# A planned kernel gets 192-column index projections, a plan in which VectorE and GpSimd exclude each other, and 64x64 products held together

## The chip, the cores and the metric

The kernel runs on one core of a Trainium2 chip. The metric is the time of one execution on the device in microseconds; the time of a kernel is the median of its runs. Besides, one execution was recorded by the profiler; spans, durations and waits below are of that one.

## The reference

Two layers work on 256 tokens of 2048 channels. Each normalises x, projects it by one wide matrix, and gives the columns to three branches: A (a Mamba-2 scan), B (RWKV-7 time mixing, a delta rule with a 64x64 state per head, 16 heads) and C (sparse attention). Gated sums of the three are projected once more and added to x. What the change touches is branch C's indexer: 16 small heads score each key for each query, and only the best top_k = 64 keys are attended to:

```python
top_k = min(TOPK_MAX, S // 4)            # 64 for S = 256
logits_idx = jnp.einsum('bqhd,bsd->bqhs', iqb, ik)
score = jnp.einsum('bqh,bqhs->bqs', iwb, jax.nn.relu(logits_idx))
score = jnp.where(causal[None], score, -jnp.inf)
_, sel = lax.top_k(score, top_k)
```

The mask is causal, so query t has t + 1 keys. Queries 0 to 63 have at most 64 and get all of them, whatever the scores.

## The kernel before

Activations lie transposed, channels on partitions and the 256 tokens along the columns. Every float32 weight and activation is split into a high and a low part (type fp32r), and a product is three: high x high, high x low, low x high (`acc`). Weights stream from memory into `wraw`, 128 x 1024 at a time; `prepare` makes halves of 512 columns from it, on ScalarE (ACT) the high part `whi` and on VectorE (DVE) `wlo = wraw - whi`. `block` runs the products of one block of 128 output channels: 16 chunks of 128 input channels, three products each, the weights stationary and `hh` or `hl`, the activations, moving. `unit` does two blocks into one PSUM tile `psg`, of which there are 3. One half of weights serves 12 products. These long products are most of TensorE's (PE's) work.

The small products of the branches go to PSUM tiles `psa` (5 of them). After each half, `pump` advances the chains ("lanes") of the branches by a step in the program's order. Branch B has for each pair of head pairs a serial part, `rwkv_chunk`: for two halves of a chunk, four 64x64 float32 products, one for each head, with the inverse (`ut`) as stationary operand; a copy of all four by ScalarE; then four with `b_nm` (the correction), which VectorE adds to X, two heads at a time. Branch C's index part: four units of index queries (`proj_c`), each rotated by `rope` on VectorE and GpSimd (POOL), then for each of the 16 heads `index_scores` on the rotated tile, and `select`, which finds the 64 best by eight rounds of max and replace. The order of units is a written string: B and C mixed, then A, then 16 merges each of C, B and A, then the output projection.

Nothing of this is issued directly. `note` records each instruction with what it depends on, and `issue` then plans: it runs clocks for PE, DVE, ACT, POOL and SP through a model of each instruction's duration (`cost`), and at each step an engine takes the first instruction by (rank, program order) whose operands are ready by these clocks, and whose tile finds a free buffer. The smaller rank goes first: -1 critical, 0 urgent (rope, evacuations), 1 weights, 2 the rest. The outcome is a fixed order for each engine; on the chip each engine takes its instructions in that order and waits for what isn't there. The clocks themselves reach the chip in no other way.

Of the kernel before, what the change touches and what calls it, by code (L numbers as in the profile page):

```python
# [11 lines left out]
F32R = mybir.dt.float32r  # L12
BF = mybir.dt.bfloat16
# [6 lines left out]
DM, S, NL = 2048, 256, 2  # L20
NK = DM // 128
OA, OB, OC, OG = 0, 3088, 7312, 10976
NEG = -1.0e30
GONE = -3.0e38
KAP = 0.5 * math.exp(-0.5)
N1, N2 = 45, 9
WB = 4
# [4 lines left out]
PG = 3  # L32
# [158 lines left out]
    return {"x": x, "post": post, "pos": pos, "par": par, "w2a2": w2a2, "wst": wst, "cst": consts()}  # L191


LP = 200
LD = 140
LT = 130
PT = 180
PO = 300
LW = 0.83
SQ = [(9,), (1, 3)]  # L200

# [1 line left out]
class Program:  # L203
# [51 lines left out]
    def note(self, eng, op, f, a, k):  # L255
        w = [k["out"] if "out" in k else a[0]] + [k[n] for n in ("accum_out",) if n in k]
        r = [x for x in list(a[("out" not in k):]) + [v for n, v in k.items() if n not in ("out", "accum_out")]
             if isinstance(x, bass.AP)]
        i = len(self.ops)
        deps = set()  # L260
        tiles = set()
        for aps, writes in ((r, False), (w, True)):
            for ap in aps:
                g = self.region(ap)
                if g[0] in self.tiles:
                    tiles.add(g[0])
                elif ap.space == bass.MemoryType.DRAM and not g[0].startswith(("diag", "out")):
                    continue
                ws, rs = self.seen.setdefault(g[0], ({}, {}))
                hit = lambda q: q[0] < g[2] and g[1] < q[1] and q[2] < g[4] and g[3] < q[3]  # L270
                deps.update(j for q, j in ws.items() if hit(q))
                if writes or ap.space == bass.MemoryType.PSUM:

                    deps.update(j for j, q in rs.items() if hit(q) and (writes or self.ops[j][0] != eng))
                    inside = lambda q: g[1] <= q[0] and q[1] <= g[2] and g[3] <= q[2] and q[3] <= g[4]
                    for q in [q for q in ws if inside(q)]:
                        del ws[q]
                    for j in [j for j, q in rs.items() if inside(q)]:
                        del rs[j]
                    ws[g[1:]] = i  # L280
                else:
                    rs[i] = g[1:]
        deps.discard(i)
        for t in tiles:
            self.tiles[t][2] += 1
        self.ops.append((eng, op, f, a, k, deps, tiles, self.rank, self.cost(eng, op, w[0], r, k), w[0].shape[0]))

    @staticmethod
    def cost(eng, op, out, r, k):

        n = int(np.prod(out.shape[1:]))
        if op == "dma_start":
            b = 4.0 * n * out.shape[0]
            return {"SP": 500.0, "ACT": 500.0, "POOL": 1050.0}[eng], b
        if eng == "PE":
            if r[0].dtype in (F32R, BF):
                return n / 2.4 + 1.7, 0.0
            if op == "transpose":
                return n / 1.2, 0.0
            return n / 0.6 * (0.4 if r[0].shape[0] <= 32 or out.shape[0] <= 32 else 0.58 if out.shape[0] <= 64 else 1.05), 0.0  # L300
        m = max([n] + [int(np.prod(x.shape[1:])) for x in r])
        ps = any(x.space == bass.MemoryType.PSUM for x in r)
        sc = sum(int(np.prod(x.shape[1:])) == 1 for x in r) if m > 1 else 0
        if eng == "ACT":
            return (51.0 if ps else 94.0) + 0.833 * m + 93.0 * min(sc, 2) + (46.0 if "accum_out" in k else 0.0), 0.0
        if eng == "DVE":
            fast = op in ("tensor_scalar", "tensor_copy") and not ps
            return 70.0 + (0.52 if fast else 1.042) * m + 61.0 * (sc > 0), 0.0
        if op in ("memset", "affine_select"):
            return 35.0 + (0.83 if op == "memset" else 1.27) * m, 0.0  # L310
        if op == "tensor_scalar":
            return 374.0 * m / 256 + 83.0 * sc, 0.0
        return PT + 2.1 * m, 0.0

    def issue(self, tc):
        ops = self.ops
# [3 lines left out]
        ready = [0.0] * N  # L320
# [3 lines left out]
                users[j].append(i)  # L324
        cand = {e: [] for e in self.ENGINES}
        add = lambda i: insort(cand[ops[i][0]], (ops[i][7], i))
        for i in range(N):
            if not left[i]:
                add(i)
# [4 lines left out]
        names = {tag: names for tag, (_, names) in self.tags.items()}  # L334
        used = {tag: 0 for tag in self.tags}
        clk = {e: 0.0 for e in self.ENGINES}
        dma = 0.0
        table = 0
        last = 200.0
# [6 lines left out]
        while len(order) < N:  # L346
            t, k, e = heappop(events)
            best = None
            later = None
            until = None  # L350
            for c in cand[e]:
                i = c[1]
                if i > front + AHEAD or until and t + ops[i][8][0] > until:
                    continue
                if ready[i] > t:
                    if c[0] < 0 and ready[i] < t + 250.0 and not until:
                        until = ready[i]
                    later = ready[i] if later is None else min(later, ready[i])
                    continue
                ok = True  # L360
                for n in ops[i][6]:
                    if first[n]:
                        tag, no = self.tiles[n][:2]
                        al, dd = alive[tag], dead[tag]
                        while dd and dd[0][0] <= t:
                            al.remove(heappop(dd)[1])
                        held = used[tag] - (len(names[tag]) - len(al))
                        room = self.tags[tag][0]
                        if held >= room or held >= room - KEEP.get(tag, room) and bisect_left(al, no) >= room:
                            ok = False  # L370
                            break
                if ok:
                    best = c
                    break
# [5 lines left out]
            idle = 0  # L380
            cand[e].remove(best)
            i = best[1]
            _, op, f, a, kw, deps, tiles, _, (busy, b), _ = ops[i]
            order.append(i)
            while front < N and end[front] is not None:
                front += 1
# [1 line left out]
                table = self.TABLES[a[2]]  # L388
                busy += 1300.0
            if e == "PE":  # L390
                w = ops[i][9]
                busy += max(0.0, LW * w - last)
                last = ops[i][8][0]
            clk[e] = t + busy
            if op == "dma_start":
                dma = max(dma, t + busy + 650.0) + b / 360.0
# [3 lines left out]
            for n in tiles:  # L400
                used[self.tiles[n][0]] += first[n]
                first[n] = False
                q = self.tiles[n]
# [4 lines left out]
            for j in users[i]:  # L408
                left[j] -= 1
                to = ops[j][0]  # L410
                ready[j] = max(ready[j], t + busy if to == e == "PE" else end[i] + (LT if to == "PE" else 0.0))
                if not left[j]:
                    add(j)
            heappush(events, (clk[e], k, e))
# [24 lines left out]
class Trunk:  # L439
# [288 lines left out]
        self.mm(out, w[0], x[1], False, False)  # L728
        self.mm(out, w[1], x[0], False, last)

    def block(self, l, out, x, nch):

        n = 8 * nch
        for k in range(n):
            if k % 4 == 0:
                w = self.half()
            self.acc(out, [None if q is None else q[:, 128 * (k % 4):128 * (k % 4) + 128] for q in w],
                     [None if q is None else q[k] if isinstance(q, list) else q[:, k, :] for q in x], k == 0, k == n - 1)
            if k % 4 == 3:
                self.pump()  # L740

    def unit(self, l, x, n=2, nch=2):
        p = self.P("g", PG).rearrange("p (b t) -> p b t", b=2)
        for i in range(n):
            self.block(l, p[:, i, :], x, nch)
        return p

    def split(self, src, hi, lo, scale=None):
# [70 lines left out]
    SWAP = [(i + 16) % 32 for i in range(32)]  # L819

    @urgent
    def rope(self, outs, x, n):

        P = x.shape[0]
        bc = lambda a: a[:P].to_broadcast([P, n, S])
        t = self.t2(2, S)[:P, :n]
        u = self.t2(2, S)[:P, :n]
        self.v.tensor_tensor(t, x, bc(self.cos), op=OP.mult)
        self.v.stream_shuffle(u, x, self.SWAP)
        self.g.tensor_tensor(u, u, bc(self.sin), op=OP.mult)  # L830
        for o in outs:
            self.g.tensor_tensor(o, t, u, op=OP.add)
# [418 lines left out]
    def select(self):  # L1251
# [6 lines left out]
        for sl in (slice(128, 384), slice(0, 128)):  # L1258
            for _ in range(8):
                yield  # L1260
                v.max(m8, sc[:, sl])
                v.match_replace(sc[:, sl], m8, sc[:, sl], GONE)
        v.tensor_scalar(sc, sc, 0.9 * GONE, NEG, op0=OP.is_gt, op1=OP.mult)
        kb = self.T([128, 384], "c_kb", 1, BF)
# [46 lines left out]
    def proj_c(self, l, h):  # L1311
        s = self.s
        p = self.unit(l, h)
# [9 lines left out]
        for k in range(16):  # L1323
            if k % 2 == 0:
                w = self.half()
# [8 lines left out]
        self.score = self.t2(384)  # L1334
        self.kb = None
        for n in range(4):
            p = self.unit(l, h)
            iq = self.t2(2, S)
            self.rope([iq], p, 2)
            self.spawn("C", self.index_scores(iq, n))  # L1340
            yield
        self.spawn("C", self.select())
        self.yc = self.T([128, 8, S], "yc")
        for n in range(4):
            p = self.unit(l, h)
            if n == 0:
                self.q = self.T([128, 8, S], "ya")
            q = self.q[:, 2 * n:2 * n + 2, :]
            self.rope([q], p, 2)
            yield  # L1350
            p = self.unit(l, h)
# [262 lines left out]
```

## Time and profile before

| | |
|---|---|
| median of 3 runs | 2407.58 us (2406.02 to 2408.8) |
| the profiled execution's own time | 2403.02 us |
| its span | 2401.3 us |
| TensorE, VectorE, ScalarE, GpSimd busy | 97%, 71%, 59%, 33% |
| products on TensorE | 18750 |

The span reaches from the first instruction to the last. All compute instructions stand under one line, 418, the one that issues what was planned; they are told apart by tiles: `psg<-hh,wlo` is a product into psg with hh moving and wlo stationary. `t` stands for the many working tiles, `zl`, `zp` and `cst` are the constants and zero-padded tiles. PEld are the loads of the stationary operands. "idle before" names what ended an engine's idle time. Each product's duration holds its way through the array, so the distance of two starts says what a product costs, not the duration.

### The profile page before, as it was taken

What the parts mean: (1) busy time and instruction counts of PE and PEld (TensorE: products, weight loads), DVE (VectorE), ACT (ScalarE), POOL (GpSimd) and SP (SyncE); (2) the same over time, 40 slices, a digit from 0 to 9 for tenths busy, and PEclk for the clock granted to TensorE, in tenths of its full rate; (3) what the DMA queues carried; (4) which work ended last, traced back from release to release, by engine and by line L of the source; (5) the groups of instructions that cost most, each with busy time, mean ns of one, the idle gap of its engine ahead of it and who ended that gap; (6) DMA issues with size and microseconds to landing.
All of it is one profiled execution on the core that took longest, in us unless ns stands there. A gap on an engine that the chain in (4) does not pass through costs nothing.

```text
span 2401.3 us, 50275 instructions
## 1 busy us (share of the span) xinstructions
PE 2330.3 (97%) x18750; PEld 2251.6 (94%) x18750; DVE 1709.5 (71%) x3468; ACT 1411.0 (59%) x2994; POOL 790.6 (33%) x1233
## 2 busy tenths in 40 slices
PE   8999999999999999999989999999999999999998
PEld 7899898999999999999879999899999999999987
DVE  8877788778885555556577778787798855555565
ACT  6766566667554454545467675666756544544453
POOL 3567565634210010101234776447351100101001
PEclk9999999999999999999999999999999999999999
DMA  5444353535545665556544544334454456655563
GB/s 188 147 153 154 114 160 99 162 118 164 162 150 185 203 221 188 197 189 212 182 133 150 164 130 153 116 126 159 123 171 144 160 186 219 208 185 194 185 212 130
DMA packets 149588, 396.14 MB, mean 165 GB/s; under 512 B 47904, under 2 KB 51936, under 8 KB 149088
## 3 DMA queue, kind: packets, MB, share of 16 engines
q1 hardware_dynamic: 149344, 392.94, 50.2%
q8 instruction: 147, 2.41, 0.4%
q14 instruction: 97, 0.79, 0.1%
HBM read 386.55 MB, written 6.32 MB: 164 GB/s over the span
## 4 chain that ended last, share of the span: by engine, by line
PE 70%; DVE 7%; ACT 3%; POOL 2%; issue 2%; ACTq 0%; DVEq 0%; POOLq 0%
PE psg L418 61%; PE psa L418 8%; DVE t L418 4%; DVE wlo L418 2%; ACT t L418 2%; POOL t L418 2%; ACT whi L418 1%; POOL zl L418 0%; DVE b_cu L418 0%; DVE n_x L418 0%; DVE b_ec L418 0%; DVE yb L418 0%; ACT b_nm L418 0%; DVE b_sc L418 0%; POOL yb L418 0%
## 5 line engine op out<-in xcount | busy, mean ns | idle before, releaser
L418 DVE TENSOR_TENSOR wlo<-wraw,whi 128x512 fp32r<-128x512 f32 x1352 | 1007.4, 746 | 567.6 <-ACT whi L418 545.2
L418 ACT ACTIVATE whi<-wraw 128x512 fp32r<-128x512 f32 x1361 | 857.4, 631 | 755.8 <-PE psg L418 700.1
L418 PE MATMUL psg<-hh,wlo 128*128 128x256 f32 x4224 | 1191.5, 282 | 3.7 <-DVE wlo L418 3.7
L418 PE MATMUL psg<-hh,whi 128*128 128x256 f32 x4224 | 1193.1, 282 | 0.0
L418 PE MATMUL psg<-hl,whi 128*128 128x256 f32 x4224 | 1186.9, 281 | 1.0 <-DVE hl L418 1.0
L418 PEld LDWEIGHTS psg<-hh,wlo 128*128 128x128 f32 x4224 | 794.9, 188 | 6.4 <-DVE wlo L418 4.9
L418 PEld LDWEIGHTS psg<-hl,whi 128*128 128x128 f32 x4224 | 796.1, 188 | 3.2 <-DVE hl L418 1.3
L418 PEld LDWEIGHTS psg<-hh,whi 128*128 128x128 f32 x4224 | 796.2, 188 | 2.1 <-issue 0.8
L418 POOL TENSOR_TENSOR t<-t,t 128x256 fp32r<-128x256 f32 (+21 forms) x506 | 338.8, 673 | 307.7 <-ACT t L418 152.8
L418 POOL TENSOR_TENSOR b_nm<-b_nm,t 128x256 f32<-128x256 f32 x64 | 48.9, 764 | 717.9 <-DVE t L418 710.2
L418 PE MATMUL psg<-t,whi 128*128 128x256 f32 x1536 | 280.8, 283 | 0.0
L418 PEld LDWEIGHTS psg<-t,whi 128*128 128x128 f32 x1536 | 238.8, 191 | 0.1
L418 ACT ACTIVATE t<-t 64x256 fp32r<-64x256 f32 (+5 forms) x436 | 179.9, 417 | 66.2 <-DVE t L418 53.7
L418 PE MATMUL psg<-t,wlo 128*128 128x256 f32 x768 | 217.2, 283 | 0.0
L418 PEld LDWEIGHTS psg<-t,wlo 128*128 128x128 f32 x768 | 147.1, 192 | 0.0
L418 ACT ACTIVATE t<-psa 128x256 f32<-128x256 f32 (+5 forms) x230 | 94.4, 426 | 38.4 <-PE psa L418 36.6
L418 POOL TENSOR_TENSOR t<-t,d 128x60 f32<-128x60 f32 (+24 forms) x248 | 104.9, 423 | 22.5 <-DMA d<-diag 6.0
L418 PE MATMUL psa<-t,t 128*128 128x256 f32 (+1 forms) x384 | 92.2, 300 | 10.1 <-ACT t L418 7.5
L418 PE MATMUL psg<-whi,hh 128*128 128x512 f32 (+1 forms) x268 | 97.9, 365 | 0.0
L418 PE MATMUL psg<-wlo,hh 128*128 128x512 f32 (+1 forms) x268 | 97.8, 365 | 0.0
L418 PE MATMUL psg<-whi,hl 128*128 128x512 f32 (+1 forms) x268 | 97.2, 365 | 0.0
L418 PE MATMUL psa<-t,zp 128*128 128x128 f32 (+1 forms) x448 | 81.8, 300 | 2.1 <-ACT t L418 2.0
(247 smaller groups left out, 2517.3 us busy)
## 6 DMA issues: line engine op xcount, KB each, us to landing
wraw<-in_wst SPq DMA_DIRECT2D x688, 512.0 KB, 3.4
d<-diag SPq DMA_DIRECT2D x32, 128.0 KB, 3.9
t<-diag SPq DMA_DIRECT2D x16, 256.0 KB, 4.0
d<-in_wst SPq DMA_DIRECT2D x8, 512.0 KB, 5.3
ya<-in_x SPq DMA_DIRECT2D x8, 256.0 KB, 5.2
yb<-in_x SPq DMA_DIRECT2D x8, 256.0 KB, 5.9
b_nm<-in_post SPq DMA_DIRECT2D x2, 1024.0 KB, 6.8
out_x<-ya SPq DMA_DIRECT2D x8, 256.0 KB, 2.8
```

Source lines behind the costliest of these rows:

```text
L418: ops[i][2](*ops[i][3], **ops[i][4])
```

## The change

1. `proj_c`: the units of the index queries are computed for the columns (queries) 64 to 255 only, `ts = slice(TOP, S)`. `unit`, `block` and `rope` take that slice. Columns 0 to 63 of the tile are set to zero by GpSimd; the scoring and the selection are the same as before, and queries 0 to 63 all get scores of zero for it.
2. `note` gives each instruction a form: for PE the shape of its stationary operand rounded up to 32, 64 or 128; for DVE whether it reads two operands of SBUF (or is a copy or tensor_scalar from SBUF); for POOL whether it is anything but a memset. In `issue` a change of the PE's form costs 90 ns; an instruction of DVE or POOL with such a form begins when the other engine's last one has ended, less 55 ns.
3. `issue` gathers successive products into the same psa tile to a batch. The first product of a batch is placed 300 ns (SLACK) after it is ready, where its rank is above 0. If its form isn't 128x128, it is also held until all that the batch needs from outside has been placed and is ready.
4. `cost` has other numbers: a 256-column product of fp32r is 118.2 ns instead of 108.4, a transpose 30, POOL's latency 200 instead of 300, and others as in the diff.

```diff
+TOP = 64
...
+SLACK = 300
+SWITCH = 90
 LP = 200
 LD = 140
 LT = 130
-PT = 180
-PO = 300
+PO = 200
...
+        form = None
+        size = lambda x: int(np.prod(x.shape[1:]))
+        sb = [x for x in r if x.space != bass.MemoryType.PSUM and size(x) > 1]
+        if eng == "PE":
+            cut = lambda n: 32 if n <= 32 else 64 if n <= 64 else 128
+            form = cut(r[0].shape[0]), cut(size(r[0]))
+        elif eng == "DVE":
+            form = size(w[0]) >= 8 and (len(sb) > 1 or len(sb) == len([x for x in r if size(x) > 1])
+                                        and op in ("tensor_scalar", "tensor_copy"))
+        elif eng == "POOL":
+            form = op != "memset"
...
             if r[0].dtype in (F32R, BF):
-                return n / 2.4 + 1.7, 0.0
+                return n * 0.442 + 5.0 if r[0].shape[0] > 64 else n / 1.2, 0.0
             if op == "transpose":
-                return n / 1.2, 0.0
-            return n / 0.6 * (0.4 if r[0].shape[0] <= 32 or out.shape[0] <= 32 else 0.58 if out.shape[0] <= 64 else 1.05), 0.0
+                return 30.0, 0.0
+            return 2 * max(n / 1.2 + 2.0, LW * int(np.prod(r[0].shape[1:]))), 0.0
...
-            return (51.0 if ps else 94.0) + 0.833 * m + 93.0 * min(sc, 2) + (46.0 if "accum_out" in k else 0.0), 0.0
+            return (51.0 if ps else 105.0) + 0.836 * m + 93.0 * min(sc, 2) + (95.0 if "accum_out" in k else 0.0), 0.0
...
-            return 35.0 + (0.83 if op == "memset" else 1.27) * m, 0.0
+            return 35.0 + (0.83 if op == "memset" else 1.32) * m, 0.0
...
-        return PT + 2.1 * m, 0.0
+        return (170.0 if m > 200 else 110.0) + 2.05 * m, 0.0
...
+        batch = {}
+        run = None
+        for i, o in enumerate(ops):
+            bank = o[0] == "PE" and o[3][0].tensor.name
+            if bank and bank.startswith("psa"):
+                if run is None or run[3] != bank or i - 1 not in batch:
+                    run = [i, 0, 0.0, bank]
+                batch[i] = run
+                run[1] += sum(batch.get(j) is not run for j in o[5])
...
-                if ready[i] > t:
+                late = ready[i]
+                if e == "PE" and i in batch:
+                    if i == batch[i][0]:
+                        if ops[i][10] != (128, 128):
+                            if batch[i][1]:
+                                continue
+                            late = batch[i][2]
+                        if c[0] > 0:
+                            late += SLACK
+                if late > t:
...
             if e == "PE":
-                w = ops[i][9]
-                busy += max(0.0, LW * w - last)
-                last = ops[i][8][0]
+                busy += SWITCH if form != cut else max(0.0, LW * ops[i][9] - last)
+                cut = form
+                last = ops[i][8][0] / (1 if ops[i][3][1].dtype in (F32R, BF) or op == "transpose" else 2)
+            elif form:
+
+                busy += max(0.0, port["POOL" if e == "DVE" else "DVE"] - t - 55.0)
+                port[e] = t + busy
...
+                if j in batch and batch.get(i) is not batch[j]:
+                    batch[j][1] -= 1
+                    batch[j][2] = max(batch[j][2], ready[j])
...
-    def unit(self, l, x, n=2, nch=2):
-        p = self.P("g", PG).rearrange("p (b t) -> p b t", b=2)
+    def unit(self, l, x, n=2, nch=2, ts=slice(0, S)):
+        p = self.P("g", PG).rearrange("p (b t) -> p b t", b=2)[:, :, ts]
...
         for n in range(4):
-            p = self.unit(l, h)
+
+            ts = slice(TOP, S)
+            p = self.unit(l, h, ts=ts)
             iq = self.t2(2, S)
-            self.rope([iq], p, 2)
+            self.g.memset(iq[:, :, 0:TOP], 0.0)
+            self.rope([iq[:, :, ts]], p, 2, ts)
             self.spawn("C", self.index_scores(iq, n))
```

More of the change, by code (lines that the diff above doesn't have):

```diff
@@ L285, in note @@
             self.tiles[t][2] += 1
-        self.ops.append((eng, op, f, a, k, deps, tiles, self.rank, self.cost(eng, op, w[0], r, k), w[0].shape[0]))
+        form = None
[9 more added lines that the diff above has]
+            form = op != "memset"
+        self.ops.append((eng, op, f, a, k, deps, tiles, self.rank, self.cost(eng, op, w[0], r, k), w[0].shape[0], form))
     @staticmethod
@@ L336, in issue @@
         clk = {e: 0.0 for e in self.ENGINES}
+        port = {"DVE": 0.0, "POOL": 0.0}
+        cut = None
         dma = 0.0
@@ L354, in issue @@
                     continue
-                if ready[i] > t:
+                late = ready[i]
[8 more added lines that the diff above has]
+                if late > t:
                     if c[0] < 0 and ready[i] < t + 250.0 and not until:
                         until = ready[i]
-                    later = ready[i] if later is None else min(later, ready[i])
+                    later = late if later is None else min(later, late)
                     continue
@@ L382, in issue @@
             i = best[1]
-            _, op, f, a, kw, deps, tiles, _, (busy, b), _ = ops[i]
+            _, op, f, a, kw, deps, tiles, _, (busy, b), _, form = ops[i]
             order.append(i)
@@ L729, in acc, with block @@
         self.mm(out, w[1], x[0], False, last)
-    def block(self, l, out, x, nch):
+    def block(self, l, out, x, nch, ts=slice(0, S)):
         n = 8 * nch
@@ L737, in block @@
             self.acc(out, [None if q is None else q[:, 128 * (k % 4):128 * (k % 4) + 128] for q in w],
-                     [None if q is None else q[k] if isinstance(q, list) else q[:, k, :] for q in x], k == 0, k == n - 1)
+                     [None if q is None else q[k] if isinstance(q, list) else q[:, k, ts] for q in x], k == 0, k == n - 1)
             if k % 4 == 3:
                 self.pump()
-    def unit(self, l, x, n=2, nch=2):
-        p = self.P("g", PG).rearrange("p (b t) -> p b t", b=2)
+    def unit(self, l, x, n=2, nch=2, ts=slice(0, S)):
+        p = self.P("g", PG).rearrange("p (b t) -> p b t", b=2)[:, :, ts]
         for i in range(n):
-            self.block(l, p[:, i, :], x, nch)
+            self.block(l, p[:, i, :], x, nch, ts)
         return p
@@ L821, in rope @@
     @urgent
-    def rope(self, outs, x, n):
+    def rope(self, outs, x, n, ts=slice(0, S)):
         P = x.shape[0]
-        bc = lambda a: a[:P].to_broadcast([P, n, S])
-        t = self.t2(2, S)[:P, :n]
-        u = self.t2(2, S)[:P, :n]
+        bc = lambda a: a[:P, :, ts].to_broadcast([P, n, ts.stop - ts.start])
+        t = self.t2(2, S)[:P, :n, ts]
+        u = self.t2(2, S)[:P, :n, ts]
         self.v.tensor_tensor(t, x, bc(self.cos), op=OP.mult)
```

## The prediction

> **What bounds the kernel now.** I read the page first, then the stages by windows, then TensorE's waits, then single products.
>
> ```profile
> span 2401.3 us, 50275 instructions
> PE 2330.3 (97%) x18750; PEld 2251.6 (94%) x18750; DVE 1709.5 (71%) x3468; ACT 1411.0 (59%) x2994; POOL 790.6 (33%) x1233
> ```
>
> TensorE (PE) is the bound: 97% busy, and the windows below grant it the full clock (1.00). Time leaves this kernel only if TensorE has less to do or waits less.
>
> ```profile
> core 0: us, PE busy (x) PEld busy (x) DVE busy (x) ACT busy (x) POOL busy (x), PEclk, DMA share, GB/s
> 60.00:720.00 660.00, 635.70 (x5255) 614.86 (x5254) 534.90 (x1192) 432.19 (x997) 337.92 (x543) 1.00 0.45 144
> 1260.00:1860.00 600.00, 579.82 (x4795) 559.26 (x4794) 471.90 (x1062) 393.19 (x914) 319.82 (x524) 1.00 0.46 144
> 780.00:900.00 120.00, 120.00 (x1015) 120.00 (x1014) 68.14 (x109) 61.28 (x109) 6.62 (x10) 1.00 0.63 211
> 1740.00:1800.00 60.00, 58.13 (x488) 57.05 (x487) 59.60 (x131) 33.21 (x66) 35.17 (x70) 1.00 0.50 166
> ```
>
> The third window lies in the merges, where only long products run: 120 us / 1015 = 0.1182 us for a product of 256 columns, with nothing lost. The first two are the branch stages of the two layers, 1260 us together, and only there is something lost. What it is, the waits of the weight loads (PEld, which run just ahead of the products) say, for the same two windows:
>
> ```profile
> PEld psa L418 <- ACT t L418: 16.6, 24, 3.6
> PEld psa L418 <- DVE t L418: 8.1, 8, 2.7
> PEld psa L418 <- POOL t L418: 4.7, 12, 1.0
> PEld psa L418 <- ACT whi L418: 2.1, 1, 2.1
> PEld psa L418 <- POOL zl L418: 1.5, 4, 0.6
> ...
> PEld psa L418 <- ACT t L418: 10.2, 19, 1.6
> PEld psa L418 <- POOL t L418: 9.5, 15, 1.4
> PEld psa L418 <- DVE t L418: 5.8, 9, 1.3
> PEld psa L418 <- ACT ut L418: 1.8, 2, 1.5
> PEld psa L418 <- POOL zl L418: 1.1, 3, 0.6
> PEld psa L418 <- ACT b_kt L418: 0.6, 2, 0.4
> ```
>
> Sum, count, longest. All are on psa, the small products of the branches: 33.0 us in 49 waits and 29.0 us in 50, so 62.0 us in 99, 0.63 us each. TensorE takes its instructions in the order that the planner wrote; when a small product is placed before its operand is there, the long products behind it (psg), which could run, wait too.
>
> **The change, part by part.** *Columns 0 to 63 of the index queries are left out.* 4 units x 2 blocks x 16 chunks x 3 products x 2 layers = 768 products go from 256 to 192 columns. No product of 192 columns is in the trace. These of 128 are nearest:
>
> ```profile
> 291.18 0.22 PE L418 MATMUL psa<-t,t 128*128 128x128 f32 x1
> 291.24 0.28 PE L418 MATMUL psa<-zl,t 128*128 128x128 f32 x1
> 291.35 0.33 PE L418 MATMUL psa<-t,t 128*128 128x256 f32 x1
> ...
> 250.98 1.95 PE L418 MATMUL psa<-t,b_nm 128*128 128x128 f32 x16
> 252.69 0.36 PE L418 MATMUL psa<-zl,t 128*128 128x256 f32 x1
> ```
>
> First column start, second duration. The first 128-column product makes way after 0.06 us (half of 0.118, so narrow products stream at the full rate), the second only after 0.11: its successor brings new weights of 128 columns, and these were not in yet. Sixteen products with 128-column weights take 252.69 - 250.98 = 1.71 us, 0.107 each. Every index product brings new weights, so I take 0.111, between these: 768 x (0.1182 - 0.111) = 5.5 us. Bounds: nothing saved, if the loads already set 0.118; and 768 x 0.1182 x 64/256 = 22.7 us, if the stream alone sets it.
>
> The Trainium skill (TensorE: Matmul & The Clock Gate, Back-to-back issue gap) gives N/2.4 + 2.5 ns for an isolated warm product; by it 256 columns take 109.2 and 192 take 82.5 ns, and the part would bring 20.5 us instead of 5.5. Its section LDWEIGHTS (loading the stationary operand) gives P/1.2, 106.7 ns for 128 columns, which speaks against that gain; the trace's 0.107 agrees with the second.
>
> *What goes with it.* Rope of an index unit now handles 384 of 512 columns, and a memset on POOL fills 2 x 64 with zeros:
>
> ```profile
> L418 DVE STREAM_SHUFFLE t<-psg 128x512 f32<-128x512 f32 x18 | 13.3, 741 | 0.1
> L418 POOL TENSOR_TENSOR t<-t,sin 128x512 f32<-128x512 f32 x18 | 28.9, 1607 | 75.8 <-DVE t L418 62.8 <-DVE c_sm L418 12.9
> L418 POOL MEMSET zl<- 128x2560 f32 x1 | 2.2, 2232 | 0.0
> ```
>
> A quarter off gives 0.19 us of DVE and 0.40 of POOL for these two rows, eight times; the memset costs 2232 x 128/2560 = 0.11 us. DVE is at 80% of the stage (534.90 + 471.90 of 1260) and POOL at 52%, so this lies beside TensorE: I count 0. If that cover went, it would still be a gain. The memset needs a free t2 buffer; behind it on POOL's queue stand rope's products and the low halves for psa, which would wait with it, and ScalarE's stack of that unit waits for it. The planner issues it only when its buffer is free by its clocks. Scores, top-k and transfers keep their instructions; columns 0 to 63 are multiplied as zeros.
>
> *64x64 products held.*
>
> ```profile
> L418 PE MATMUL psa<-t,ut 64*64 64x64 f32 x256 | 28.2, 230 | 2.5 <-ACT ut L418 1.3 <-DVE t L418 1.1
> L418 PE MATMUL psa<-zp,b_nm 64*64 64x64 f32 x128 | 10.8, 224 | 0.0
> ...
> 502.91 0.28 PE L418 MATMUL psg<-hl,whi 128*128 128x256 f32 x1
> 503.12 0.44 PE L418 MATMUL psa<-t,ut 64*64 64x64 f32 x4
> 503.49 0.38 PE L418 MATMUL psg<-hh,wlo 128*128 128x256 f32 x1
> 503.71 0.28 PE L418 MATMUL psg<-hh,whi 128*128 128x256 f32 x1
> ...
> 494.95 0.28 PE L418 MATMUL psa<-t,t 128*128 128x256 f32 x1
> 495.16 0.68 PE L418 MATMUL psa<-zp,b_nm 64*64 64x64 f32 x8
> 495.76 0.39 PE L418 MATMUL psa<-zl,t 128*128 128x256 f32 x1
> 495.99 0.28 PE L418 MATMUL psa<-t,t 128*128 128x256 f32 x1
> ```
>
> An f32 product leaves two records, so four heads make eight. The correction (zp,b_nm) runs as 16 visits of eight; the inverse (t,ut) as 64 visits of four, two heads and then two more (the first at 255.00, the last at 1833.74). A visit of four takes 503.71 - 502.91 - 2 x 0.118 = 0.56 us, one of eight 495.99 - 494.95 - 0.236 = 0.80: entering and leaving the 64x64 shape is most of it. Joining 32 pairs saves 32 x (2 x 0.56 - 0.80) = 10.2 us. The hold costs no chain: the ScalarE copy behind it reads all four anyway, and long products fill the gap. Bound below: 0, if the halves stay apart.
>
> *The planner's costs and SLACK.* No instruction goes; the order changes. The first product of each psa group (rank above 0) is placed 300 ns after the planner thinks it ready, and waits of DVE on POOL and back are now planned. Those waits exist:
>
> ```profile
> L418 DVE TENSOR_TENSOR wlo<-wraw,whi x1352: 661/693/1785, 27.4 to 2367.3; 128x512 fp32r<-128x512 f32 x194
> L418 POOL TENSOR_TENSOR zl<-t,t x76: 722/780/1517, 38.8 to 1704.4; 64x256 fp32r<-64x256 f32 x76
> ```
>
> Minimum, median, maximum: the same instruction takes over twice as long at times, and the old planner knew nothing of it, so results came late and TensorE stood. With 0.3 us more, each of the 99 waits shrinks by up to 0.3: at most 29.7 us. Short ones give only their own length; I take four fifths, 24 us, since the mean of 0.63 lets most be longer than 0.3. Above that: all 62.0 us, if the new costs are exact. Below: 0, or a loss (first rival). Against it stands that a 256-column product was planned at 256/2.4 + 1.7 = 108.4 ns and is now 118.2: long products placed to cover a wait used to cover 9% more than planned, and that hidden margin goes. The chains get later by 0.3 us a step, and have room:
>
> ```profile
> L418 DVE SCALAR_TENSOR_TENSOR yb<-t,yb x16: 407/414/525, 295.9 to 1862.8; 128x256 f32<-128x256 f32 x16
> ```
>
> Branch B's last result of layer 2 is there at 1862.8, and its merges come after the 16 of branch C, which alone are 16 x 72 x 0.1182 = 136 us of products. The first work to be late, if any, would be wlo on DVE, with 0.75 us for each 12 products (1.42 us).
>
> Sum: 5.5 + 10.2 + 24 = 40 us. The profiled execution took 2403.0 us (span 2401.3), the median is 2407.6: 2401.3 - 40 = 2361 of span, 2403.0 - 40 = 2363 for such an execution, and 2368 against the median.
>
> **The rivals.**
> - *Just in time is too late (slower).* The 9% margin beats 0.3 us where a small product's operand takes over 0.3/0.09 = 3.3 us from its last product, as the eight DVE steps of an inverse root may. If waits grow by 0.25 us each instead: +25 - 16 = +9, 2417 us. It decides from 16 us of added wait, 0.16 on each of the 99. For it: the waits on ACT (26.8 us) have no contention to be corrected. Against: in the code most operands are one or two instructions behind the product before.
> - *Waits only move.* The work saved stays, 16 us: 2392. For it: 1740 to 1800, where DVE is busy 59.60 of 60 us and TensorE cannot gain. Against: 80% over the stage.
> - *The stream sets 192 columns*, if a load of weights starts early enough to hide behind two products: 22.7 instead of 5.5, 2351. Against: the 0.11 before new weights. The Trainium skill's formula for the gap, above, is this rival's rule.
> - *Waits nearly vanish*: 55 instead of 24 us, 2337.
> - *The halves stay split*, so the hold doesn't do what it says: 2378. I hold that unlikely and keep it within the forecast.
>
> **How the numbers follow.** Forecast (2350 to 2385) 0.46; stream 0.08; waits vanish 0.12; waits only move 0.16; near no change 0.06; slower 0.12. Faster by over 0.2% (4.8 us, about what a measurement of this kernel can tell) is the first four, 0.82. The range 2335 to 2410 leaves out the low tail of the fourth and the slower cases.
>
> **What would show it.** Index products of 192 columns starting 0.111 apart; t,ut in 32 visits of eight; PEld's psa waits near 38 us in the branch stages, and their windows shorter by some 20 us each; the merges at 0.118 as before. Wrong would be: waits of 60 us or more, or waits on DVE's wlo for psg.

## The result, and the profile after

The changed kernel takes 2333.2 us (2330.53 to 2334.52, 4 runs) against 2407.4 before: 0.969 of it, 95% interval 0.9674 to 0.9707. That is 74 us less, nearly twice the forecast of 40, and 2 us under the range. The page of the changed kernel, its span, busy times and one group:

```profile
span 2332.1 us, 50202 instructions
PE 2295.8 (98%) x18750; PEld 2239.0 (96%) x18750; DVE 1712.8 (73%) x3468; ACT 1405.9 (60%) x2994; POOL 797.6 (34%) x1241
L460 DVE TENSOR_TENSOR wlo<-wraw,whi 128x512 fp32r<-128x512 f32 x1352 | 1018.6, 756 | 528.3 <-ACT whi L460 515.6
```

As many products, DVE and ACT instructions as before, 8 more on POOL (the memsets). TensorE is busy for less time and a larger share. Where the 69.2 us of span went is seen from three marks in the timeline of TensorE (start, duration, operation): the first product of the merges (t,whi) in each layer and, between them, the first projection product of layer 2 (hh,whi). Before, then after:

```profile
703.17 0.39 PE L418 MATMUL psg<-t,whi 128*128 128x256 f32 x2
1213.86 0.36 PE L418 MATMUL psg<-hh,whi 128*128 128x256 f32 x1
1897.57 0.48 PE L418 MATMUL psg<-t,whi 128*128 128x256 f32 x2
...
665.11 0.40 PE L460 MATMUL psg<-t,whi 128*128 128x256 f32 x2
1176.73 0.44 PE L460 MATMUL psg<-hh,whi 128*128 128x256 f32 x1
1826.81 0.39 PE L460 MATMUL psg<-t,whi 128*128 128x256 f32 x2
```

The first branch stage ends 38.1 us earlier. From there to layer 2's first projection it is 511.6 instead of 510.7, from there to the second merges 650.1 instead of 683.7, 33.6 less, and from these to the end 505.3 instead of 503.7. So all of it lies in the two stretches that hold the branch stages. Their waits, those of the weight loads in 60 to 660 and in 1215 to 1785 us (sum, count, longest):

```profile
PEld psa L460 <- POOL t L460: 1.8, 6, 0.8
PEld psa L460 <- ACT zp L460: 1.5, 2, 0.8
PEld psa L460 <- DVE t L460: 1.5, 3, 0.7
PEld psa L460 <- POOL zl L460: 1.5, 2, 1.1
PEld psa L460 <- ACT t L460: 1.3, 4, 0.5
PEld psa L460 <- ACT b_kt L460: 1.0, 2, 0.5
...
PEld psa L460 <- DVE t L460: 4.8, 3, 3.8
PEld psa L460 <- ACT t L460: 3.0, 5, 0.9
PEld psa L460 <- DVE adt L460: 1.9, 1, 1.9
```

With 2.1 us more in six single or paired waits of the second window that are not shown, it is 20.4 us in 34 waits; before it was 62.0 in 99. (Both leave out the rows under *issue*, for which the profile names no releaser, and waits of psg.) The waits on ACT t, 26.8 us in 43 before, are 4.3 in 9. Not only are they shorter: two thirds are gone. The loads for psg waited too, before in the two windows, then after in the second:

```profile
PEld psg L418 <- DVE wlo L418: 1.7, 2, 1.3
PEld psg L418 <- DVE wlo L418: 1.4, 2, 0.8
...
PEld psg L460 <- DVE wlo L460: 0.2, 1, 0.2
```

Each wait also cost something behind it. Four index products before, the first time on the heels of a long product, the second after a wait of their load:

```profile
142.90 0.28 PE L418 MATMUL psg<-hh,wlo 128*128 128x256 f32 x1
143.01 0.62 PE L418 MATMUL psa<-t,t 128*128 128x128 f32 x4
143.47 0.28 PE L418 MATMUL psg<-hh,whi 128*128 128x256 f32 x1
...
145.00 0.28 PE L418 MATMUL psg<-hh,whi 128*128 128x256 f32 x1
145.33 0.73 PE L418 MATMUL psa<-t,t 128*128 128x128 f32 x4
145.90 0.28 PE L418 MATMUL psg<-hl,whi 128*128 128x256 f32 x1
...
145.33 0.52 PEld L418 LDWEIGHTS psa<-t,t 128*128 128x128 f32 x4 [0.26 <-POOL t L418]
```

From the long product ahead to the one behind it is 0.57 us undisturbed and 0.90 with the wait: 0.33 more, of which the load's row tells 0.26. In the eleven such groups with a wait in this trace the part that the row doesn't tell is 0.06 us each, so 65 waits less make an estimate of 4 us. The two parts that save work are as forecast:

```profile
1296.82 0.25 PE L460 MATMUL psg<-hl,whi 128*128 128x192 f32 x1
...
1306.07 0.35 PE L460 MATMUL psa<-t,t 128*128 128x128 f32 x2
...
1776.14 0.27 PE L460 MATMUL psg<-hl,whi 128*128 128x256 f32 x1
1776.35 0.67 PE L460 MATMUL psa<-t,ut 64*64 64x64 f32 x8
1776.95 0.39 PE L460 MATMUL psg<-hh,wlo 128*128 128x256 f32 x1
1777.18 0.28 PE L460 MATMUL psg<-hh,whi 128*128 128x256 f32 x1
```

Between the first two rows lie 83 products of 192 columns: 9.25 / 83 = 0.1114 us each, so 768 x (0.1182 - 0.1114) = 5.2 us. The inverse runs in 32 visits of eight, the last at 1776.35. So the account of 69: waits on psa 41.6, on psg 2.9, what follows them 4, visits 10.2, columns 5.2, together 64; some 5 us are not assigned.

### The profile page after: what moved, and what is told of

It reads as the page before. It is cut to its first block, busy times and chain, and to the rows that moved or that the text cites. A ratio compares the mean times of both kernels' runs of the same rounds, so it can differ in the third digit from the quotient of the medians.

```text
span 2332.1 us, 50202 instructions
## 1 busy us (share of the span) xinstructions
PE 2295.8 (98%) x18750; PEld 2239.0 (96%) x18750; DVE 1712.8 (73%) x3468; ACT 1405.9 (60%) x2994; POOL 797.6 (34%) x1241
## 5 line engine op out<-in xcount | busy, mean ns | idle before, releaser
L460 DVE TENSOR_TENSOR wlo<-wraw,whi 128x512 fp32r<-128x512 f32 x1352 | 1018.6, 756 | 528.3 <-ACT whi L460 515.6
L460 PE MATMUL psg<-hh,whi 128*128 128x256 f32 (+1 forms) x4224 | 1190.5, 282 | 1.0 <-ACT hh L460 1.0
L460 PE MATMUL psg<-hh,wlo 128*128 128x256 f32 (+1 forms) x4224 | 1190.1, 282 | 0.0
L460 PE MATMUL psg<-hl,whi 128*128 128x256 f32 (+1 forms) x4224 | 1186.6, 281 | 0.0
L460 POOL TENSOR_TENSOR t<-t,t 128x256 fp32r<-128x256 f32 (+22 forms) x506 | 340.5, 676 | 283.0 <-ACT t L460 170.4
L460 PE MATMUL psa<-t,t 128*128 128x256 f32 (+1 forms) x384 | 87.5, 288 | 2.8 <-ACT t L460 2.2
```

Of the source, the lines that this page charges most:

```text
L460: ops[i][2](*ops[i][3], **ops[i][4])
```

## The experiments

Three theories run through the expectations. S: SLACK does it. C: a planner whose clocks are nearer the chip's does it, part by part. M, made after the first eight runs: the clocks must be right together. Times are medians; ratios are to the kernel before, run on the same chip, where it took 2407.0 to 2408.1. Waits are those of the weight loads for psa in the two branch stages, without the rows under *issue*.

**One part taken out of the changed kernel (2333.2).** No slack:

```diff
-SLACK = 300
+SLACK = 0
```

> The changed kernel with SLACK = 0. Theory S (the 300 ns do it): most of the fallen waits come back, 2365 to 2385 us, psa waits of the weight loads in the branch stages over 45 us. Theory C (clocks that match the chip do it, the costs and the port rule): up to 10 us over the changed kernel, 2333 to 2343 us, waits near 25 us.

2346.7 us (0.9745, 0.9729 to 0.976): +13.5. More than C allowed, far less than S: SLACK is not the main part. The waits are 29.1 us in 57, nearer to C's 25 than to S's 45: without SLACK, the new clocks already hold them at half of what they were.

The old `cost` and POOL latency, and no charge for a switch:

```diff
-                return n * 0.442 + 5.0 if r[0].shape[0] > 64 else n / 1.2, 0.0
+                return n / 2.4 + 1.7, 0.0
...
-                busy += SWITCH if form != cut else max(0.0, LW * ops[i][9] - last)
+                busy += max(0.0, LW * ops[i][9] - last)
```

> The changed kernel with the old costs of all engines (and no charge for a switch of shape), but SLACK, hold, port rule and 192 columns. Theory S: within 10 us of the changed kernel, 2328 to 2343. Theory C: 2355 to 2375, for the clocks of TensorE run 9% fast again. A third view, that the old costs' hidden margin of 9% adds to SLACK: below 2333.

2395.8 us (0.9946, 0.9931 to 0.9961): +62.5, more than C's figure. The margin does not add to SLACK.

The port rule (point 2 of the change: VectorE and GpSimd exclude each other in the plan) taken out:

```diff
-            elif form:
+            elif False:
```

> The changed kernel without the port rule (VectorE and GpSimd don't delay each other in the plan). Theory S: within 8 us, 2330 to 2341. Theory C: 2345 to 2370, with more waits on POOL and DVE.

2455.9 us (1.0197, 1.018 to 1.0213): +122.7, slower than the kernel before, though its products save 15 us of work. No theory had this.

The hold taken out:

```diff
-                        if ops[i][10] != (128, 128):
+                        if False:
```

> The changed kernel without the hold: 64x64 products go as soon as the first is ready. Both theories: 32 more visits of the 64x64 shape at 0.32 us, so about +10 us, 2340 to 2346. If the hold also kept TensorE from waits inside a group of four, more than that: 2350 or over.

2331.1 us (0.9677, 0.9658 to 0.9697): no change that can be told. Here only 28 visits are of four and 34 of eight, so 14 more visits in all, 4.5 us. In its trace the waits are 15.1 us in 29 against 20.4 in 34, 5.3 less, which about makes up for them.

**One part put into the kernel before (2408.1).** SLACK alone, on the first product of each psa group:

```diff
+SLACK = 300
...
-                if ready[i] > t:
+                late = ready[i]
+                if e == "PE" and i in batch:
+                    if i == batch[i][0]:
...
+                        if c[0] > 0:
+                            late += SLACK
+                if late > t:
```

> The kernel before with SLACK = 300 as the only edit. Theory S: 2407 less 35 to 50, 2357 to 2372 us, psa waits of the weight loads in the branch stages down from 62 to under 25 us. Theory C: less 5 to 20, 2387 to 2402, as the operands still come later than the clocks say.

2390.3 us (0.993, 0.9916 to 0.9945): -18, C's side. In the windows of the prediction (60 to 720 and 1260 to 1860) its waits are 49.1 us in 97, where S had under 25. The largest rows of each:

```profile
PEld psa L460 <- ACT t L460: 9.4, 18, 1.5
PEld psa L460 <- POOL t L460: 8.1, 16, 1.0
PEld psa L460 <- DVE t L460: 5.7, 8, 2.7
...
PEld psa L460 <- ACT t L460: 9.5, 19, 2.0
PEld psa L460 <- POOL t L460: 6.0, 13, 1.1
PEld psa L460 <- DVE t L460: 3.4, 5, 1.0
```

Nearly as many waits as before (99), and 12.9 us less in them.

The new costs and the port rule (all of `cost` and of the clocks in the diff above):

```diff
+                return n * 0.442 + 5.0 if r[0].shape[0] > 64 else n / 1.2, 0.0
...
+            elif form:
+
+                busy += max(0.0, port["POOL" if e == "DVE" else "DVE"] - t - 55.0)
+                port[e] = t + busy
```

> The kernel before with the new costs, the charge for a switch of shape and the port rule, but no SLACK, no hold and 256 columns. Theory C: 2357 to 2375 us. Theory S: 2395 to 2420, since the 9% margin is gone too.

2378.0 us (0.9882, 0.9867 to 0.9896): -30, the largest single part, short of C's figure by 3 us. In the same windows the waits are 26.5 us in 51, so that about half are gone. Beside them stands one of 17.0 us under *issue*; the row of its product (waits of PE) names a transfer:

```profile
PE psa L460 <- DMA vd<-diag: 17.1, 2, 16.8
```

`vd` gets the diagonal blocks of branch B's inverse, which GpSimd works out. So with the new clocks alone a product can still stand far too early. Without this one wait the run would take an estimated 2361 us, within C's figure.

The 192 columns:

```diff
+            ts = slice(TOP, S)
+            p = self.unit(l, h, ts=ts)
```

> The kernel before with 192 columns in the index units as the only edit. The step of the prediction says 5.5 us less, 2402; if the order that it shifts matters, anywhere within 10 us of that.

2399.1 us (0.9964, 0.9952 to 0.9977): -9, with an interval from -5.5 to -11.6; the 5.2 of the columns lies just outside of it, so the order it shifts gave a little.

The hold:

```diff
+                        if ops[i][10] != (128, 128):
+                            if batch[i][1]:
+                                continue
+                            late = batch[i][2]
```

> The kernel before with the hold as the only edit: 10.2 us less by the visits, 2397 us, with 48 visits of eight; more, 2385 or lower, if waits inside the groups of four fall as well.

2400.8 us (0.9967, 0.9954 to 0.9979): -7, 48 visits of eight, as forecast within the interval (-5 to -11).

Singly the parts give 18 + 30 + 9 + 7 = 64 of 74. But inside the second something must cancel: the changed kernel without its port rule is slower than the kernel before, and without its new costs only 12 us faster.

**What the clocks must be.** Old costs and no port rule, with SLACK, hold and 192 columns:

> The changed kernel with the old costs and without the port rule, so the old clocks throughout, with SLACK, hold and 192 columns. Theory M (the clocks must be right together: too fast a TensorE hid too fast a VectorE and GpSimd): about 2408 - 18 - 9 - 7 = 2374 us, better than with only the port rule taken out (2456) or only the old costs put in (2396). Theory A (each part has its own effect): 2333 + 123 + 62 = 2518.

2378.4 us (0.9877, 0.9863 to 0.9892): M's figure within 5, and 140 below A's. Two edits that cost 62 and 123 us one by one cost 45 together. The two errors of the old clocks cancel in part.

TensorE's old costs alone (the two lines above and its transposes and float32 products):

> The changed kernel with the old costs for TensorE alone. Theory M: these carry the loss of the old costs, 2375 to 2400 us, with long products waiting for VectorE to free their tile. If the other engines' costs carry it: under 2345.

2378.4 us (0.9875, 0.986 to 0.989): +45 of the 62: TensorE's costs alone make up most of it.

Then the counterparts, put into the kernel before: the lines of TensorE in `cost` with the charge for a switch, and the three lines of the port rule, each by itself.

```diff
-                return n / 2.4 + 1.7, 0.0
+                return n * 0.442 + 5.0 if r[0].shape[0] > 64 else n / 1.2, 0.0
```

> The kernel before with TensorE's new costs (and the charge for a switch of shape) alone. Theory M: it takes the margin and leaves VectorE and GpSimd too fast in the plan, so slower, 2430 to 2490 us. Theory C in its plain form (a clock nearer the chip's is better): 2385 to 2405.

2460.7 us (1.0219, 1.0202 to 1.0236): +53, as M had it.

```diff
+                busy += max(0.0, port["POOL" if e == "DVE" else "DVE"] - t - 55.0)
```

> The kernel before with the port rule alone, on the old costs. Theory M: VectorE is now right but TensorE fast in the plan, so waits for small products fall and long waits for VectorE's evacuations come, as in the changed kernel with old costs: 2395 to 2430 us. Plain theory C: 2370 to 2390.

2481.5 us (1.0308, 1.0288 to 1.0327): +73, more than M had. With the new costs of the other engines too, the two together gave -30. The waits over the whole run: TensorE's new costs alone; then the port rule alone, its weight loads, its VectorE and its products:

```profile
PEld psa L460 <- ACT t L460: 45.5, 62, 2.8
PEld psa L460 <- DVE t L460: 22.4, 24, 3.2
PEld psa L460 <- POOL t L460: 20.8, 47, 1.0
...
PEld psa L460 <- issue: 38.4, 17, 15.4
PEld psg L460 <- DVE yc L460: 19.9, 4, 13.3
PEld psg L460 <- DVE t L460: 15.5, 5, 8.3
PEld psa L460 <- DVE t L460: 11.2, 8, 6.3
...
DVE t L460 <- PE psa L460: 91.2, 48, 31.3
...
PE psa L460 <- DMA vd<-diag: 32.3, 3, 15.1
```

A plan in which VectorE and GpSimd are too fast makes many short waits of small products, 0.4 to 0.9 us each in these rows. In the branch stages they are 156 here and 144 in the changed kernel without the port rule, against about 100 before.

The port rule with the old TensorE costs makes few and long ones. The largest are for the inverse, 32.3 us in three. VectorE's longest wait for a small product (31.3 us; 2.3 at most before) lies around one of these: it stands from 1635.77 to 1667.09, TensorE from 1643.35 to 1658.49. At the longest wait of the long products, 13.1 us from 373.32 on, VectorE is busy for 11.2 us, with branch C's selection and what follows it. So chains of the helpers come late; how the fast TensorE of the plan brings that about is not shown step by step. A long wait costs more than its length. Behind that one the granted clock is half (the 0.50 in the first row), and the products start 0.21 us apart instead of 0.118:

```profile
386.38:389.00 2.62, 2.62 (x12) 2.62 (x13) 0.00 (x0) 0.00 (x0) 0.73 (x1) 0.50 0.00 0
386.76 0.41 PE L460 MATMUL psg<-hl,whi 128*128 128x256 f32 x1
386.98 0.41 PE L460 MATMUL psg<-hh,wlo 128*128 128x256 f32 x1
```

**Mean speed, or when they meet?** No port rule, but flat factors:

```diff
-            return 70.0 + (0.52 if fast else 1.042) * m + 61.0 * (sc > 0), 0.0
+            return 1.19 * (70.0 + (0.52 if fast else 1.042) * m + 61.0 * (sc > 0)), 0.0
...
-        return (170.0 if m > 200 else 110.0) + 2.05 * m, 0.0
+        return 1.3 * ((170.0 if m > 200 else 110.0) + 2.05 * m), 0.0
```

> The changed kernel without the port rule, but VectorE's costs times 1.19 and GpSimd's (memsets apart) times 1.3 at all times, the mean of what the trace of before shows over each shape's 5th percentile. Theory M in its simple form (mean speed is what counts): 2335 to 2350 us. If it matters when the two engines meet: over 2380.

2374.8 us (0.9868, 0.9851 to 0.9885), between the two: these factors give back 81 of the 123 us, and 42 are left. Other factors were not tried, so how much of the 42 is due to when the two engines meet is not settled.

**SLACK as a remedy.** `SLACK = 1200` without the port rule:

> The changed kernel without the port rule and with SLACK = 1200. If without the rule small products are merely placed too early by up to a microsecond, SLACK makes up for it: 2340 to 2370 us. If the order on VectorE and GpSimd themselves is what suffers: above 2400.

2438.4 us (1.0128, 1.0109 to 1.0147): only 17 of the 123, the second reading's side. Placing the small products 0.9 us later does not mend it: over the run the waits on ACT t fall from 41.2 us to 11.3, and those on POOL t rise from 24.3 to 43.7.

With the port rule, SLACK of 600 and of 1200:

> The changed kernel with SLACK = 600. Theory S: another 5 to 12 us less, 2321 to 2328. Theory C: the clocks are near, and the waits that are left are not of this kind: within 5 us of 2333.

2330.4 us (0.9672, 0.9657 to 0.9688), within what C expected.

> The changed kernel with SLACK = 1200. If SLACK only covers the planner's error: 2325 to 2335 us, nothing more to win than with 600. If the longer steps make a chain late: above 2340.

2323.2 us (0.9649, 0.9633 to 0.9664): 10 less than the changed kernel, 2 below what was expected, 7 below SLACK 600, where nothing more was expected, and the fastest version run here. No chain came too late. What more SLACK wins with the new clocks is small; where it ends was not tried.

## Why the prediction was right or wrong

- What bounds it: right. The time went from TensorE's waits on small products and its own work, in the branch stages alone, and the merges run as before. Not quite all waits were on psa: 3.1 us in four were loads for psg, on wlo.
- 192 columns: 0.111 forecast, 0.1114 measured. The stream alone would take 0.1182 x 192 / 256 = 0.089, and of the 705 distances between two such products in the trace only 38 are 0.091 or less; the rival by which the stream sets the pace is out. That the loads set it is what is left, one for each product, but it was not isolated. There was luck in the figure: the 0.107 of the sixteen products is a mean, which the last of them lowers. The others start 0.112 apart, and they are float32, whose stream alone may set that (at 256 columns such a record takes 0.215).
- On these products the Trainium skill's two rules (TensorE: Matmul & The Clock Gate, Back-to-back issue gap and LDWEIGHTS) fare differently: the load of 128 columns in P/1.2 = 106.7 ns is near the 0.1114 us, the gap of 82.5 ns is not reached.
- The hold: 32 visits of eight and 0.80 us each, as forecast; alone it gives 7 of the 10.2 us, with the waits as before. In the changed kernel, though, taking it out costs nothing that can be told.
- **The planner's costs and SLACK: this step failed.** The sum gave the whole gain to SLACK: each of 99 waits shrinks by up to 0.3 us, at most 29.7, taken as 24. The new costs and the port rule were nothing in the sum; they stood only in the bound "all 62.0 us, if the new costs are exact". Both halves were wrong. SLACK alone shortens the waits by 12.9 us, 0.13 each, and takes next to none of them away. The new costs with the port rule alone take half of them away (26.5 us in 51). In time, SLACK gives 18 alone and 13.5 at the end; the costs with the port rule 30 alone and 45 at the end. The step as a whole gave 74 less 15, 59 us, where the sum had 24.
- Why the clocks do more than a margin is a reading, not shown: a margin moves a product later by the same amount everywhere, while a clock that is wrong for one engine shifts the order on all of them.
- The signs: waits near 38 us, and they are 20.4; each stage some 20 us shorter, and they are 38.1 and 33.6. Waits of wlo for psg, the sign of being wrong, were there before and fell to 0.2.
- The rival *waits nearly vanish* (55 us, 2337, chance 0.12) came nearest in time, by luck: 41.6 of the waits went, not 55, and the rest came from the waits on psg, from what follows a wait, and from what is not assigned.
- The rival *just in time is too late* fits one half of the change. TensorE's new costs, which take the 9% margin away, alone make the kernel 53 us slower, more than the rival's price. What the prediction did not see is that the port rule gives it back. It had both rows before it: the 9% of a product, and wlo at 661 to 1785 ns.
- *Waits only move*, for VectorE at 59.60 of 60 us: did not come. VectorE is busy for 517 of 600 us in the first branch stage after, and TensorE 595:

```profile
60.00:660.00 600.00, 594.87 (x5081) 585.15 (x5080) 517.39 (x1140) 419.45 (x968) 333.21 (x538) 1.00 0.48 154
```

## What to carry to other kernels

Where a plan in software fixes each engine's order, mind the ratio of its clocks before anything else. Here two errors that cancelled in part were better than one of them mended, and a part of such a change judged alone had the wrong sign (+53 and +73 for parts that, with the other engines' costs, bring -30). In the waits, many short ones for small operands went with helpers planned too fast. Long ones have no such plain sign: they came with TensorE planned too fast, but one of 16.8 us also with all the new costs; follow them to the product's own row and to what its chain waited for. Slack comes after the clocks: with the port rule missing, 900 ns more of it won back 17 of 123 us.

## What the runs showed of the hardware

VectorE's instructions stretch when GpSimd works beside them. Of the 1352 wlo before, the 871 that no GpSimd instruction overlaps take 667 to 694 ns, the other 481 up to 1785. The plan counts this and does not avoid it: wlo takes 756 ns in the mean after and took 746 before; GpSimd is busy for 797.6 us and was for 790.6, with a quarter less to rotate in the index units. The spread of wlo is the same, that of zl smaller (minimum, median, maximum):

```profile
L460 DVE TENSOR_TENSOR wlo<-wraw,whi x1352: 626/692/1782, 29.5 to 2298.2; 128x512 fp32r<-128x512 f32 x194
L460 POOL TENSOR_TENSOR zl<-t,t x76: 717/741/1282, 39.2 to 1651.1; 64x256 fp32r<-64x256 f32 x76
```

A visit to the 64x64 shape costs 0.56 us for four records (two float32 products) and 0.80 for eight, so that the shape itself, in and out, is an estimated 2 x 0.56 - 0.80 = 0.32 us of it.
